# Rotating q and k out of PSUM before their norm, with shared roots and a float32 turn

## The chip, the cores and the metric

The kernel runs on one core of a Trainium2 chip. The metric is the device time of one execution in microseconds (us); lower is better. A core has TensorE (PE in the profile: matmuls and transposes; PEld is its weight load), VectorE (DVE), ScalarE (ACT), GpSimd (POOL) and the queue SP, which issues the DMA transfers. Each engine works through its own instructions in order and waits for others by semaphores. Matmuls write to PSUM; all other on-chip data is in SBUF.

## The reference, cut to what matters

One encoder layer on 1024 tokens of width 1024: a feed-forward half step, a mixer (attention beside a state-space scan), a second feed-forward half step and a gated embedding. The change is in the projection that feeds attention:

```python
u = x @ w_in[i]
q, k, v, z, xs, bm, cm, dt_raw = jnp.split(u, SPLIT_POINTS, axis=-1)
qf = _rms(q.reshape(B, S, N_Q_HEADS, HEAD_DIM).astype(jnp.float32), q_norm[i])
kf = _rms(k.reshape(B, S, N_KV_HEADS, HEAD_DIM).astype(jnp.float32), k_norm[i])
qh = _apply_rope(qf, cos, sin).astype(x.dtype)
kh = _apply_rope(kf, cos, sin).astype(x.dtype)

def _rms(xf, w):
    return xf * lax.rsqrt(jnp.mean(jnp.square(xf), axis=-1, keepdims=True) + RMS_EPS) * w
def _apply_rope(xf, cos, sin):            # pairs (x0, x1) of a head
    return jnp.stack([x0 * c - x1 * s, x0 * s + x1 * c], axis=-1).reshape(xf.shape)
```

There are 8 heads of q and 2 of k, each 64 wide. The factor of the norm is one number per token and head, so it can be multiplied in before or after the rotation; the weight of the norm is folded into the tables of sines and cosines.

## The kernel before, in words

All matmuls are done at float32 precision as three products of halves: a value is split into a high part of type float32r and the rest, `lo = value - hi` (the helper `lo`, line 87, on VectorE; the high part is a ScalarE copy), and `mm3` (lines 116 to 123, the matmul is L122) issues three matmuls for each block of 128 rows of the contraction.

`in_proj` calls `qkv_part`. Its loops run over 8 tiles of 128 tokens, first for q (`qq`, 24 matmuls of 512 columns a tile), then for k, v and dt (`kv`, 24 matmuls of 272 columns a tile). After the matmuls of tile t, `step` (lines 916 to 927) does in this order: the turn of an older tile out of the list `late`; the front of tile t (`norm`: Square on ScalarE L848, sum over each head L850, mean and epsilon L851, the root as a power of -0.5 on GpSimd L853); the low half of an older tile (L87); and the back of tile t-1 (`rope`: one Newton step on the root in `newton`, L129 to L132; the product with the root read from PSUM L860; the rotation L866 to L868; then the ScalarE copy to a high half L903 or L886).

The turn brings a tile from tokens on the partitions to head elements on the partitions. Before the change it transposes the halves: for each q head one 128x128 transposition of 64 high and 64 low columns together (L909, 8 a tile), and one copy into Q (L910); for k two heads by two halves, each written twice side by side (L892, 4 a tile), and one copy into K (L893). In Q[:, h] the upper 64 partitions hold the high half and the lower 64 the low half. K[:, g, 0] holds the high half of k on both halves of the partitions, K[:, g, 1] the low half on both, so that attention's two matmuls a product (L1159) form all four products of halves.

TensorE's order is fixed by the program: `layer.in_order` chains every TensorE instruction to the one before. The other engines' orders are made when the kernel is compiled, by a planner that walks a simulated timeline and gives each engine the instruction that is ready and comes earliest in the program. The orders are then fixed. Tiles in SBUF and PSUM come from pools with a given number of buffers; a new tile waits until the last reader of the buffer's old contents is done. Two pools of PSUM matter here: `big` (2 buffers of 1024 columns, `psb`) and `sm` (4 buffers of 512 columns, `pss`).

`kv_weights` loads and splits the weights of k and v during the last two q tiles. `tables` makes the rotation tables, two VectorE instructions (L842) and two small loads, for q ahead of its loop and for k behind the first k tile. What the step leaves over for k is put into the list `pend`, from which `xbc_gemm` pops two entries after each half of the next projection (`x0`, 2 times 24 matmuls of 512 columns, in a `big` buffer). Behind it comes `xbc_part`: a convolution out of PSUM (ScalarE L972, four VectorE taps L977, Silu L984 for each of 8 blocks), whose scratch lies where `qkv_part`'s scratch pool `qwork` lay.

Of the kernel before, what the change touches and what calls it, by code (L numbers as in the profile page):

```python
# [18 lines left out]
P = 128  # L19
# [7 lines left out]
HD = 64  # L27
# [9 lines left out]
class Layer:  # L37
# [786 lines left out]
    def qkv_part(self, c, xT):  # L824
# [20 lines left out]
        def norm(ps, nh):  # L845
            v = ps.rearrange("p (h d) -> p h d", d=HD)
            sq = wk.tile([P, nh, HD], F32, name="sq")
            nc.scalar.activation(out=sq, in_=v, func=AF.Square)  # L848
            ss = self.small.tile([P, 16], F32, name="ss")[:, :nh]
            nc.vector.reduce_sum(ss, sq, axis=AX.X)  # L850
            nc.vector.tensor_scalar(out=ss, in0=ss, scalar1=1.0 / HD, scalar2=RMS_EPS, op0=ALU.mult, op1=ALU.add)  # L851
            r = self.small.tile([P, 16], F32, name="qr")[:, :nh]
            nc.gpsimd.tensor_tensor(out=r, in0=ss, in1=self.mhalf[:, :nh], op=ALU.pow)  # L853
            return v, nh, sq, ss, r

        def rope(v, nh, m, ss, r, nm, t):

            self.newton(r, ss, nh)
            qn = wk.tile([P, nh, HD], F32, name="qn")
            nc.vector.tensor_tensor(out=qn, in0=v, in1=r.unsqueeze(2).broadcast_to([P, nh, HD]), op=ALU.mult)  # L860
            T1, T2 = (x[:, t] for x in T[nm])
            H2 = HD // 2
            for a in range(2):
                o = slice(a * H2, (a + 1) * H2)
                i = slice((1 - a) * H2, (2 - a) * H2)
                nc.vector.tensor_tensor(out=m[:, :, o], in0=qn[:, :, i], in1=T2[:, o].unsqueeze(1).broadcast_to([P, nh, H2]), op=ALU.mult)  # L866
            nc.vector.tensor_tensor(out=qn, in0=qn, in1=T1.unsqueeze(1).broadcast_to([P, nh, HD]), op=ALU.mult)
            nc.vector.tensor_tensor(out=qn, in0=qn, in1=m, op=ALU.add)  # L868
            return qn

        NK = NKV * HD
        late = []

        def kv_front(t, ps):
            nc.vector.tensor_tensor(out=self.dt[:, t], in0=ps[:, 256:272], in1=dtb, op=ALU.add)
            vv = ps[:, NK:2 * NK].rearrange("p (g d) -> p g d", d=HD)
            st = norm(ps[:, :NK], NKV)
            nc.scalar.copy(out=V[:, t, :, 0], in_=vv)
            self.lo(V[:, t, :, 1], vv, V[:, t, :, 0])
            return st  # L880

        def kv_back(t, st):

            kn = rope(*st, "k", t).unsqueeze(2).broadcast_to([P, NKV, 2, HD])
            kd = wk.tile([P, NKV, 2, 2, HD], F32R, name="qs", bufs=4)
            nc.scalar.copy(out=kd[:, :, 0], in_=kn)  # L886

            def turn():
                pt = self.pss().rearrange("p (g j t) -> p g j t", g=NKV, j=2)
                for g in range(NKV):  # L890
                    for j in range(2):
                        nc.tensor.transpose(out=pt[:, g, j], in_=kd[:, g, j].rearrange("p a d -> p (a d)").bitcast(F32), identity=self.ident)  # L892
                nc.scalar.copy(out=K[:, :, :, t * P:(t + 1) * P], in_=pt)  # L893
            late.append(turn)
            return kd[:, :, 1], kn, kd[:, :, 0]

        def q_front(t, ps):
            return norm(ps, NQ)

        def q_back(t, st):  # L900
            qs = wk.tile([P, NQ, 2, HD], F32R, name="qs", bufs=4)
            qn = rope(*st, "q", t)
            nc.scalar.copy(out=qs[:, :, 0], in_=qn)  # L903

            def turn():
# [1077 lines left out]
```

## Time and profile before

| | before |
|---|---|
| median of 3 runs | 1948.35 us (1947.01 to 1949.08) |
| the profiled execution's own time | 1948.74 us |
| its span, first to last instruction | 1946.9 us |
| granted TensorE clock | 0.998 |
| PE busy | 1927.9 us, 99% of the span |
| DVE busy | 1528.0 us, 78% |
| ACT busy | 881.1 us, 45% |
| POOL busy | 416.9 us, 21% |

The stage of the change runs from about 700 us (first q matmul) to 789 us (last k transposition) of the span. The profile's views used here are the page, the chain of waits in order of time, the busy times by window, the groups of instructions by line, the instructions of one line, the timeline of one engine, and who waited for whom. In a group's row the shapes are output <- input, partitions x elements, then the count; behind the bar stand the busy time in us, the mean of one in ns, and the engine's idle time just before them. In the chain of waits and in the timeline the first number is the start and the second the duration, in us from the span's start.

### The profile page before, as it was taken

Reading aid. Unit: us, or ns where it says so; the run is one execution under the profiler, and the core shown is the slowest. Engines: PE = TensorE matmul, PEld = TensorE weight load, DVE = VectorE, ACT = ScalarE, POOL = GpSimd, SP = SyncE. Lnnn points to the kernel's source line nnn. Section 1 sums busy time; section 2 is a strip of 40 time slices with the busy share of each in tenths; the row PEclk is TensorE's granted clock in tenths of the full one; section 3 lists DMA queues with packets and bytes.
Section 4 is the critical chain, followed back from the end, with each engine's and each line's share of the span. In section 5 each row is a group of like instructions: output and inputs, shape, how many; then the busy total and the mean of one; then the engine's idle time right before and its main releaser. Section 6 shows DMA issues by size and latency. Waiting matters only on the chain.

```text
span 1946.9 us, 25645 instructions
## 1 busy us (share of the span) xinstructions
PE 1927.9 (99%) x9132; PEld 1607.8 (83%) x9132; DVE 1528.0 (78%) x2356; ACT 881.1 (45%) x1509; POOL 416.9 (21%) x310
## 2 busy tenths in 40 slices
PE   8999999999999999999999999999999999999998
PEld 6888888888888889888888888888888888888886
DVE  7977777767678668758998878997787787877698
ACT  6433333325444224537887876633333333443311
POOL 0144535430001032001221001013444440001011
PEclk9999999999999999999999999999999999999999
DMA  8434554549866111231002663244545439976022
GB/s 296 143 125 151 190 179 156 190 159 373 297 221 212 63 42 50 84 119 68 7 1 77 212 222 121 90 165 156 190 163 178 173 121 358 331 262 226 32 77 97
DMA packets 147713, 310.34 MB, mean 159 GB/s; under 512 B 18128, under 2 KB 30800, under 8 KB 147584
## 3 DMA queue, kind: packets, MB, share of 16 engines
q1 hardware_dynamic: 147584, 308.69, 45.4%
q8 instruction: 72, 1.18, 0.2%
q14 instruction: 57, 0.47, 0.1%
HBM read 217.21 MB, written 91.42 MB: 159 GB/s over the span
## 4 chain that ended last, share of the span: by engine, by line
PE 94%; DVE 3%; DMA 1%; ACT 1%; issue 1%; POOL 0%; SPq 0%; DVEq 0%; ACTq 0%
PE sm L122 59%; PE big L516 12%; PE sm L516 9%; PE big L122 3%; PE big L1159 3%; PE sm L1181 2%; PE sm L1196 1%; PE sm L1197 1%; DMA yd<-y 1%; DVE nm L1166 1%; DVE conv L977 1%; PE sm L1270 0%; PE big L224 0%; PE sm L224 0%; PE big L909 0%
## 5 line engine op out<-in xcount | busy, mean ns | idle before, releaser
L122 PE MATMUL sm<-xh,blk 128*128 128x512 f32 x1424 | 439.8, 389 | 0.0
L122 PEld LDWEIGHTS sm<-xh,blk 128*128 128x128 f32 x1424 | 267.3, 188 | 55.4
L122 PE MATMUL sm<-xl,blk 128*128 128x512 f32 x736 | 283.8, 389 | 0.0
L122 PE MATMUL sm<-blk,xl 128*128 128x512 f32 (+2 forms) x784 | 238.2, 371 | 0.2 <-ACT xn_t L1010 0.2
L122 PE MATMUL sm<-blk,xh 128*128 128x512 f32 (+2 forms) x584 | 203.3, 379 | 1.6 <-DVE acc L1466 1.1
L108 ACT CAST blk<-raw 128x512 fp32r<-128x512 f32 (+1 forms) x168 | 101.3, 611 | 215.0 <-PE sm L122 134.1
L87 DVE TENSOR_TENSOR blk<-s,blk 128x512 fp32r<-128x512 f32 x176 | 150.8, 861 | 35.2 <-ACT blk L108 33.2
L87 DVE TENSOR_TENSOR blk<-raw,blk 128x512 fp32r<-128x512 f32 (+1 forms) x168 | 146.5, 875 | 40.6 <-ACT blk L108 40.1
L108 ACT CAST blk<-s 128x512 fp32r<-128x512 f32 x172 | 105.7, 622 | 146.5 <-PE sm L122 118.3
L122 PEld LDWEIGHTS sm<-blk,xl 128*128 128x128 f32 x784 | 142.8, 188 | 24.2 <-ACT xn_t L1010 0.5
L122 PEld LDWEIGHTS sm<-xl,blk 128*128 128x128 f32 x736 | 138.2, 188 | 28.6
L178 POOL TENSOR_TENSOR ln_k<-ln_k,mhalf 128x1 f32<-128x1 f32 x32 | 37.4, 1173 | 579.2 <-DVE ln_k L177 563.0
L516 PE MATMUL big<-xh 128*128 128x512 f32 x576 | 138.8, 390 | 0.0
L267 POOL TENSOR_TENSOR s<-raw 128x512 f32<-128x512 f32 x34 | 55.0, 1617 | 387.2 <-DVE blk L87 381.7
L87 DVE TENSOR_TENSOR xh<-blk,xh 128x1024 fp32r<-128x1024 f32 x78 | 95.4, 1223 | 48.4 <-ACT xh L462 42.3
L462 ACT CAST xl<-blk 128x1024 fp32r<-128x1024 f32 x76 | 80.2, 1055 | 113.5 <-PE sm L516 43.7
L462 ACT CAST xh<-blk 128x1024 fp32r<-128x1024 f32 x78 | 82.3, 1055 | 108.1 <-PE big L516 49.9
L122 PEld LDWEIGHTS sm<-blk,xh 128*128 128x128 f32 x584 | 109.9, 188 | 21.3 <-DVE acc L1466 1.4
L516 PEld LDWEIGHTS big<-xh 128*128 128x128 f32 x576 | 107.8, 188 | 22.2
L87 DVE TENSOR_TENSOR xl<-blk,xl 128x1024 fp32r<-128x1024 f32 x76 | 92.7, 1220 | 41.3 <-ACT xl L462 36.7
L516 PE MATMUL big<-xl 128*128 128x512 f32 x480 | 115.8, 390 | 0.0
L122 PE MATMUL sm<-xET2h,blk 128*128 128x512 f32 x352 | 108.4, 389 | 0.0
(343 smaller groups left out, 4018.5 us busy)
## 6 DMA issues: line engine op xcount, KB each, us to landing
raw<-in_wi_dram SPq DMA_DIRECT2D x81, 512.0 KB
blk<-hS SPq DMA_DIRECT2D x154, 256.0 KB
hS<-h SPq DMA_DIRECT2D x88, 256.0 KB
wr<-in_wo_dram SPq DMA_DIRECT2D x44, 512.0 KB
blk<-wT SPq DMA_DIRECT2D x88, 256.0 KB
hS<-sg SPq DMA_DIRECT2D x66, 256.0 KB
wT<-wr SPq DMA_DIRECT2D x66, 256.0 KB
blk<-in_wo_dram SPq DMA_DIRECT2D x66, 256.0 KB
```

The lines of the kernel that those rows point to most:

```text
L87: (eng or self.nc.vector).tensor_tensor(out=out, in0=full, in1=hi.bitcast(F32), op=ALU.subtract)
L108: self.nc.scalar.copy(out=b[:, 0, :n], in_=src)
L122: self.nc.tensor.matmul(ps, lhsT=a, rhs=b, start=(i == 0), stop=(i == n - 1))
L178: nc.gpsimd.tensor_tensor(out=r, in0=v, in1=self.mhalf[:, :1], op=ALU.pow)
L267: lambda: G.tensor_tensor(out=s1, in0=a21, in1=a22, op=ALU.add),
L462: A.copy(out=b[:, :, 0], in_=r)
L516: nc.tensor.matmul(ps[q], lhsT=b[:, 0, x, cut], rhs=b[:, 1, y], start=j == i == 0, stop=j == NP - 1 and i == 2)
L977: nc.vector.scalar_tensor_tensor(out=a[:, o], in0=ps[:, o.start + d - c:o.stop + d - c], scalar=cw[:, j, tap:tap + 1], in1=a[:, o], op0=AL ...
L1159: nc.tensor.matmul(ps[:, n * 512:(n + 1) * 512], lhsT=Q[:, h, q0:q0 + P], rhs=K[:, h // 4, j, n * 512:(n + 1) * 512], start=j == 0, stop=j ...
L1166: nc.vector.tensor_reduce(out=nm, in_=ps, axis=AX.X, op=ALU.max, negate=True)
L1181: nc.tensor.transpose(out=pt[:, k], in_=pr[:, kk * P:(kk + 1) * P], identity=self.ident)
L1196: nc.tensor.matmul(po, lhsT=vw, rhs=pth[k // 4][:, k % 4], start=k == 0, stop=False)
```

## The change

The order of the arithmetic changes: the unnormed q is rotated straight out of PSUM (`rope` now takes the PSUM tile), and the norm's factor is multiplied in afterwards. For q this is done by ScalarE, one instruction for each head (8 a tile); the root is taken once for two tiles (16 columns). For k, four tiles are copied to SBUF (`kraw`) and then squared, summed, rooted, rotated and scaled together (8 columns of roots, 512 columns of data); the scaling of k is one VectorE product.

The turn (`turned`) now transposes the float32 values, two heads in one 128x128 transposition: 4 a tile for q, 4 for each group of four tiles for k. The split into halves comes behind it: two ScalarE copies out of PSUM, one for each half of the partitions, and two VectorE subtractions in the step behind (`rest`). In Q the odd heads now have their high half on the lower partitions. For k the halves are then copied to the other half of the partitions by two more ScalarE copies (`then`).

The sequence is three lists. `behind`, in each step after the rotation, first runs what is left of the last turn (`los`), then the scaling of a finished group (`ready`). The scaling puts the turns into `late`, and `before`, ahead of the next step's front, takes one. So q tiles 0 and 1 are scaled in step 2 and turned in steps 4 and 5; q tiles 6 and 7 are scaled in the first k step and turned in the third and fourth; the first four k tiles are scaled in k step 4 (of 0 to 7) and turned in step 6, the last four in the pops of `x0`. The rotation table of k is made ahead of the k loop. The scratch pool's tiles change: `qs` (4 buffers) goes, `qn` has 6 buffers, and `rot`, `kraw` and `kn` come in. In the diff a longer run of removed lines is left out; the functions before stand above.

```diff
                 nc.vector.scalar_tensor_tensor(out=t_, in0=a, scalar=scale, in1=b.unsqueeze(1).broadcast_to([P, NT, HD]), op0=ALU.mult, op1=ALU.mult)
             T[nm] = (T1, T2)
 
...
+        H2, NK = HD // 2, NKV * HD
+        rows = [slice(r * HD, (r + 1) * HD) for r in range(2)]
+        Vec = nc.vector
+
+        def rope(out, v, tabs):
+            m = wk.tile([P, *v.shape[1:]], F32, name="rot")
+            flat = len(v.shape) == 3
+            T1, T2 = (x.unsqueeze(1 if flat else 2) for x in tabs)
             for a in range(2):
...
+                o, i = (slice(x * H2, (x + 1) * H2) for x in (a, 1 - a))
+                Vec.tensor_tensor(out=m[..., o], in0=v[..., i], in1=T2[..., o].broadcast_to([P, *v.shape[1:-1], H2]), op=ALU.mult)
+            Vec.tensor_tensor(out=out, in0=v, in1=T1.broadcast_to([P, *v.shape[1:]]), op=ALU.mult)
+            Vec.tensor_tensor(out=out, in0=out, in1=m, op=ALU.add)
+
+        def squares(v, ss):
+            sq = wk.tile([P, NQ, HD], F32, name="sq")
+            nc.scalar.activation(out=sq.rearrange("p h d -> p (h d)"), in_=v, func=AF.Square)
+            Vec.reduce_sum(ss, sq, axis=AX.X)
+
+        def root(ss, n):
+            ss = ss[:, :n]
+            Vec.tensor_scalar(out=ss, in0=ss, scalar1=1.0 / HD, scalar2=RMS_EPS, op0=ALU.mult, op1=ALU.add)
+            r = self.small.tile([P, 16], F32, name="qr")[:, :n]
+            nc.gpsimd.tensor_tensor(out=r, in0=ss, in1=self.mhalf[:, :n], op=ALU.pow)
+
+            def scales():
+                self.newton(r, ss, n)
+                return r
+            return scales
+
+        ready, late, los = [], [], []
+
+        def turned(pt, blocks, hi, lo, then=None):
+
+            for i, b in enumerate(blocks):
+                nc.tensor.transpose(out=pt[:, i * P:(i + 1) * P], in_=b, identity=self.ident)
+            src = [pt[rows[e]].rearrange("p (i t) -> p i t", t=P) for e in range(2)]
+            for e in range(2):
+                nc.scalar.copy(out=hi[e], in_=src[e])
+
+            def rest():
+                for e in range(2):
+                    self.lo(lo[e], src[e], hi[e])
+                if then:
+                    then()
+            los.append(rest)
+
+        def before():
+            if late:
+                late.pop(0)()
+
+        def behind():
+            if los:
+                los.pop()()
+            if ready:
+                ready.pop(0)()
+
+        kept = []
+
+        def q_turn(t, qn):
+            Qv = Q.rearrange("p (i e) s -> p i e s", e=2)[:, :, :, t * P:(t + 1) * P]
+            hi, lo = ([Qv[rows[e ^ j], :, e] for e in range(2)] for j in range(2))
+            turned(self.psb()[:, :512], [qn[:, 2 * i:2 * i + 2].rearrange("p h d -> p (h d)") for i in range(4)], hi, lo)
+
+        def q_step(t, ps):
+            before()
+            if t % 2 == 0:
+                kept.append(self.small.tile([P, 16], F32, name="ss"))
+            ss = kept[0]
+            squares(ps, ss[:, t % 2 * 8:t % 2 * 8 + 8])
+            qn = wk.tile([P, NQ, HD], F32, name="qn", bufs=6)
+            rope(qn, ps.rearrange("p (h d) -> p h d", d=HD), [x[:, t] for x in T["q"]])
+            kept.append(qn)
+            behind()
+            if t % 2:
+                _, *qns = kept
+                kept.clear()
+                scales = root(ss, 16)
+
+                def scale():
+                    r = scales()
+                    for j, q in enumerate(qns):
+                        for h in range(NQ):
+                            nc.scalar.activation(out=q[:, h], in_=q[:, h], func=AF.Identity, scale=r[:, j * 8 + h:j * 8 + h + 1])
+                    late.extend([lambda: None] * (not late) + [lambda t=t - 1 + j, q=q: q_turn(t, q) for j, q in enumerate(qns)])
+                ready.append(scale)
+
+        def kv_step(t, ps):
+            before()
+            h = t // 4
+            Vec.tensor_tensor(out=self.dt[:, t], in0=ps[:, 256:272], in1=dtb, op=ALU.add)
             vv = ps[:, NK:2 * NK].rearrange("p (g d) -> p g d", d=HD)
-            st = norm(ps[:, :NK], NKV)
+            if t % 4 == 0:
+                kept.append(wk.tile([P, 4, NK], F32, name="kraw"))
+            kr = kept[0]
+            nc.scalar.copy(out=kr[:, t % 4], in_=ps[:, :NK])
             nc.scalar.copy(out=V[:, t, :, 0], in_=vv)
             self.lo(V[:, t, :, 1], vv, V[:, t, :, 0])
...
+            behind()
+            if t % 4 == 3:
+                kept.clear()
+                ss = self.small.tile([P, 16], F32, name="ss")
+                squares(kr.rearrange("p t d -> p (t d)"), ss[:, :8])
+                scales = root(ss, 8)
+                kn = wk.tile([P, 4, NKV, HD], F32, name="kn")
+                rope(kn, kr.rearrange("p t (g d) -> p t g d", d=HD), [x[:, 4 * h:4 * h + 4] for x in T["k"]])
+                k8 = kn.rearrange("p t g d -> p (t g) d")
+                Kv = K[:, :, :, h * 512:(h + 1) * 512]
+                hi, lo = ([Kv[rows[g], g, j].rearrange("p (i t) -> p i t", t=P) for g in range(2)] for j in range(2))
+
+                def then():
+                    for g in range(2):
+                        nc.scalar.copy(out=Kv[rows[1 - g], g], in_=Kv[rows[g], g].bitcast(F32))
+
+                def scale():
+                    r = scales()
+                    Vec.tensor_tensor(out=k8, in0=k8, in1=r.unsqueeze(2).broadcast_to([P, NQ, HD]), op=ALU.mult)
+                    late.extend([lambda: None, lambda: turned(self.pss(), [kn[:, i].rearrange("p g d -> p (g d)") for i in range(4)], hi, lo, then)])
+                ready.append(scale)
 
         tables("q", HD ** -0.5)
         for t in range(NT):
             ps = self.qq(t, xT)
             if t >= NT - 2:
                 self.kv_weights(t - NT + 2)
-            step(t, ps, q_front, q_back)
+            q_step(t, ps)
+        tables("k", 1.0)
         for t in range(NT):
...
+            kv_step(t, self.kv(t, xT))
+        self.pend += [behind, before, before, behind]
         self.x0 = self.xbc_gemm(0, xT, 1)
-        assert not late and not backs and not los
+        assert not late and not ready and not los
 
     def xbc_weights(self, j):
         return [b.rearrange("p l (k c) -> p l k c", c=P) for b in self.wload(self.I["wx"][j])]
```

More of the change, by code (lines that the diff above doesn't have):

```diff
@@ L843, in tables @@
             T[nm] = (T1, T2)
[L845 to L862, printed above, removed]
-            for a in range(2):
[L864 to L869, printed above, removed]
@@ L879, in kv_front @@
             self.lo(V[:, t, :, 1], vv, V[:, t, :, 0])
[L880 to L905, printed above, removed]
-                pt = self.psb().rearrange("p (h t) -> p h t", t=P)
-                qv = qs.bitcast(F32)
-                for hh in range(NQ):
-                    nc.tensor.transpose(out=pt[:, hh], in_=qv[:, hh].rearrange("p a d -> p (a d)"), identity=self.ident)
-                nc.scalar.copy(out=Q[:, :, t * P:(t + 1) * P], in_=pt)
-            late.append(turn)
-            return qs[:, :, 1], qn, qs[:, :, 0]
```

20 lines of the change are left out of this document (removed).

## Prediction

> **What bounds the kernel now.** The page comes first, with the busy shares.
>
> ```profile
> span 1946.9 us, 25645 instructions
> PE 1927.9 (99%) x9132; PEld 1607.8 (83%) x9132; DVE 1528.0 (78%) x2356; ACT 881.1 (45%) x1509; POOL 416.9 (21%) x310
> ```
>
> PE leaves 19 us of the span, so a PE instruction taken away is worth its time as long as PE doesn't wait instead. Whether PE waits now, around the change, is in the view of who waited for whom, here PE from 700 to 960 us:
>
> ```profile
> PE sm L1119 <- ACT xn_t L1010: 0.4, 1, 0.4
> PE sm L1181 <- DVE xh L87: 0.3, 2, 0.2
> PE big L1159 <- ACT pr L1168: 0.2, 1, 0.2
> PE sm L122 <- ACT xn_t L1010: 0.2, 1, 0.2
> ```
>
> None of it lies in the stage itself. The chain of waits in order of time gives PE's pace there (start, duration):
>
> ```profile
> 741.30 5.46 PE sm L122 x24
> 746.76 0.87 PE big L909 x8
> 747.63 6.08 PE sm L122 x48
> ...
> 757.60 0.87 PE big L909 x8
> 758.47 3.01 PE sm L122 x24
> ...
> 772.29 0.44 PE sm L892 x4
> 772.73 3.01 PE sm L122 x24
> 776.18 5.47 PE big L122 x24
> ...
> 791.51 1.11 ACT conv L972
> ```
>
> A q tile is 5.46 us of matmuls, a k tile 3.01, and eight transpositions 0.87, so 0.109 each. Behind `x0` the chain leaves PE for the convolution.
>
> **The change part by part: TensorE.** The two lines' own rows count the transpositions:
>
> ```profile
> L909 PE MATMUL big<-ident,qs x64: 270/272/273, 721.2 to 762.1; 128*128 128x128 f32 x64
> L892 PE MATMUL sm<-ident,qs x32: 270/272/273, 765.2 to 788.6; 128*128 128x128 f32 x32
> ```
>
> q goes from 64 to 32, k from 32 to 8. The new ones have the same shape and type, so 56 fewer at 0.109 is 6.1 us. (I use the pace, not the 0.272 us that one takes from start to end, because they overlap.)
>
> [...]
>
> **VectorE, ScalarE and the root, in the steady state.** Rows of the groups by line, 700 to 800 us, then single lines' rows, and single rows of the timelines of ACT, POOL and DVE:
>
> ```profile
> L866 DVE TENSOR_TENSOR sq<-qn,T 128x256 f32<-128x256 f32 x16 | 6.1, 420 | 0.2
> L860 DVE TENSOR_TENSOR qn<-sm,qr 128x512 f32<-128x512 f32 x8 | 5.5, 691 | 0.7
> L868 DVE TENSOR_TENSOR qn<-qn,sq 128x512 f32<-128x512 f32 x8 | 5.5, 689 | 0.1
> L850 DVE TENSOR_REDUCE ss<-sq 128x8 f32<-128x512 f32 x8 | 5.5, 683 | 4.3 <-ACT sq L848 4.2
> L851 DVE TENSOR_SCALAR ss<-ss 128x8 f32<-128x8 f32 x8 | 1.3, 165 | 0.0
> L129 DVE TENSOR_TENSOR rs_t<-qr 128x8 f32<-128x8 f32 x8 | 1.3, 166 | 5.3 <-POOL qr L853 5.0
> L848 ACT ACTIVATE sq<-sm 128x512 f32<-128x512 f32 x8 | 4.8, 599 | 20.7 <-PE sm L122 20.7
> ...
> L1203 ACT COPY a_raw<-sm x16: 577/581/587, 906.3 to 1065.0; 64x512 f32<-64x512 f32 x16
> L1204 DVE TENSOR_TENSOR a_raw<-sm,a_raw x16: 669/689/696, 907.5 to 1065.6; 64x512 f32<-64x512 f32 x16
> ...
> 1076.47 2.04 ACT L1264 ACTIVATE xs<-xb,sdt 128x64 f32<-128x64 f32 x8
> 706.78 1.65 POOL L853 TENSOR_TENSOR qr<-ss,mhalf 128x8 f32<-128x8 f32 x1 [0.64 <-DVE ss L851]
> 723.64 2.06 POOL L853 TENSOR_TENSOR qr<-ss,mhalf 128x8 f32<-128x8 f32 x1 [3.72 <-DVE ss L851]
> 749.81 3.21 POOL L853 TENSOR_TENSOR qr<-ss,mhalf 128x8 f32<-128x8 f32 x1 [5.18 <-DVE ss L851]
> 754.53 0.70 POOL L853 TENSOR_TENSOR qr<-ss,mhalf 128x2 f32<-128x2 f32 x1 [1.50 <-DVE ss L851]
> ...
> 708.47 0.17 DVE L129 TENSOR_TENSOR rs_t<-qr 128x8 f32<-128x8 f32 x1 [1.83 <-POOL qr L853]
> 709.07 0.17 DVE L132 TENSOR_TENSOR qr<-qr,rs_t 128x8 f32<-128x8 f32 x1
> ```
>
> A new q tile costs VectorE the sum 0.68, the rotation 2.22 (two of 0.42, the product with T1 read from PSUM at L860's 0.69, the addition 0.69), two low halves on 64 partitions at L1204's 0.69 (partitions don't shorten it), and half of a mean step and four Newton steps, 0.42: 4.7 us. ScalarE pays Square 0.60, two copies at L1203's 0.58, and eight scalings with a factor per head, which L1264 does in the very form: 2.04 for eight. That is 3.8. PE's tile becomes 5.46 + 0.44 = 5.9, so both stay covered; uncovered, the scalings alone would cost 2.0 a tile.
>
> The root is now 16 columns. From 2 columns at 0.70 and 8 at 2.06, a straight line gives 3.9. The bounds come from the same line through 1.65 and through 3.21: 2.9 and 6.6. I take 3.9, since most q roots stand near 2.06.
>
> The root of 1.65 fell where VectorE did nothing but wait for it (its 1.83 of idle time ahead of L129); the others ran beside VectorE's work. [...]
>
> In the steady state all this has time: tile t of an even-odd pair ends its matmuls, and the pair's first turn is due three q tiles later, 3 x 5.9 less the last turn, 17.3 us. The q loop should run without a wait.
>
> **The border between q and k.** There the three tiles in between are k tiles. Counted from the last matmul of q tile 7, PE does three turns of 0.44 (tiles 3, 4, 5) and three k tiles of 3.01, and then wants tile 6: due at 10.35 us. What has to happen by then: Square 0.8 with its start; sum 0.68; rotation 2.22; low halves of tile 3, 1.38; mean 0.17 (all four ahead of it or beside it in the program); root 3.9; four Newton steps 0.8 at L129's 0.17 and the gaps between; eight scalings 2.04. Together 12.0, with hand-overs 12.2. PE's order is fixed, so it stands still for 1.9 us, and everything behind it on PE with it. ScalarE is not free either. By the same chain the sixteen scalings of the pair 4, 5 run from 10.2 to 14.3 us behind tile 5's last matmul, and tile 7's last is 11.8 behind that; its Square, ready at 0.2, would start at 2.5, 2.3 late. Of that 1.4 comes back, because the low halves of tile 3 are done meanwhile: 0.9. **Stall: 2.8 us.** Low bound 0: the mean taken straight behind the sum and a root of 2.9 make 7.4. High bound: Square behind all sixteen scalings and the two copies of a turn (4.1 + 1.2 + 0.6 instead of 0.8, less 1.4) with a root of 6.6 make 18.6, 8.3 late. Tile 7 follows: its scalings end 2.0 behind tile 6's, its turn is due 3.4 behind. The last k weights, and the k table's two products of 0.69 with two small loads on SP, now stand ahead of the first k tile; if that tile starts late, tile 6 is due later by as much, so nothing is added for them.
>
> **k and the tail.** The first group's chain (Square, sum, mean, root of 8, Newton, one product) takes by the same rows 0.6 + 0.68 + 0.17 + 2.06 + 0.8 + 0.69 = 5.0 and a short copy, and is due after three k tiles, 9.0: covered. The work that goes is a k tile's norm and rotation in small pieces; VectorE has less to do. The second group's turn stays the last thing in `x0`. Behind it ScalarE gets two 64-partition copies (1.16) and later two of 64x1024 for `then`, which I price by this row:
>
> ```profile
> L910 ACT CAST Q<-big 128x1024 fp32r<-128x1024 f32 x8 | 8.1, 1017 | 4.1 <-PE big L909 4.1
> ```
>
> That is 2.0 us on ScalarE, with the first convolution behind it. The convolution's taps leave ScalarE room behind it, so most is hidden; PE was 0.4 us short there already (the first row of waits), and it arrives 0.44 earlier by four transpositions. Bounds: -0.4 (that wait goes too) and 1.0 (half of the 2.0 ahead of the convolution). I take 0.3.
>
> **Sum**, against the profiled execution of 1948.74 us (1.84 around the span): -6.1 + 2.8 + 0.3 = -3.0, so 1945.7. That execution stood 0.4 above the median of the runs; against 1948.35 the forecast is **1945.3 us**.
>
> **Rivals.** (A) *No stall at the border.* For it: VectorE loses about 1 us a tile of k work, so the rows of the border may follow closer than I sum them. Against it: 12.2 against 10.35. Then -6.1 + 0.3, or from -6.5 to -5.1 with the tail's bounds: 1942.5 (1941.9 to 1943.3). [...]
>
> (B) *The border eats nearly all of it.* A root at the pace of the one at 749.81, which stood exactly there, adds 2.7: 5.5 + 0.3 - 6.1 = -0.3, 1948.0. For it: that row. Against it: the other q roots.
>
> (C) *Slower.* One mechanism: the chain from a pair's last matmul to its scaling outgrows what the turns allow, because Square queues behind sixteen scalings and the root is slow. It decides at the border from a stall of 5.8, a chain of 16.2 us; from 17.3 on the pairs before pay too. At the high bound's 18.6: the border 8.3, two earlier pairs 1.3 each, 10.9 + 0.3 - 6.1 = 5.1 more, 1953.4. Against it: it needs the worst row of each.
>
> (D) *PE gains nothing*, because what a run of transpositions costs is its change of operands and not their number. Four of L892 in 0.44 beside eight in 0.87 speak against it. It would be 2.8 + 0.3 more, 1951.4.
>
> **How the numbers follow.** Forecast 0.44 (stall 1 to 4.5: 1943.5 to 1947.0), A 0.24, B 0.17, C and D 0.15. What this measurement can tell from no change is about 0.2%, 3.9 us, so faster means below 1944.45. A lies there wholly, of the forecast's span about 0.36: 0.24 + 0.16 = 0.40. B and the rest of the forecast are the same: 0.17 + 0.28 = 0.45. C and D: 0.15. The range leaves out only C and D: 1941.6 to 1950.0, with 0.3 below A and up to a stall of 7.
>
> **What would show it.** Right: 40 transpositions of q and k; a q tile's pace of 5.9 us with no wait; PE waiting 2 to 3 us for scaled q (written by ScalarE) ahead of tile 6's turn, behind a root near 3.9; the first convolution within 1 us of its place behind `x0`. Wrong: a wait of PE within the q loop; a root over 5 us; scalings slower than 0.26 each; a wait behind 800 us that isn't there now, which would mean that fixed orders changed where nothing was edited.

## The result, and the profile after

| | before | after |
|---|---|---|
| median | 1947.96 us (4 runs beside it, 1947.01 to 1949.08) | 1958.63 us (4 runs, 1957.89 to 1960.00) |
| ratio | | 1.0056, 95% interval 1.0044 to 1.0067 |
| span of the profiled execution | 1946.9 us | 1956.6 us |
| granted TensorE clock | 0.998 | 0.996 |

The kernel after is slower by 10.7 us; the forecast was 1945.3. Of all the executions reported here and below, one (of the kernel before with four buffers for `y`) was slow, 2785.25 us at a granted clock of 0.655, and is in no ratio. The page says at once that the loss isn't work, since PE is busy 1.2 us less than before in a span that is 9.7 longer:

```profile
span 1956.6 us, 25498 instructions
PE 1926.7 (98%) x9076; PEld 1603.7 (82%) x9076; DVE 1516.4 (78%) x2266; ACT 891.1 (46%) x1566; POOL 413.5 (21%) x300
```

The transpositions are gone as the change says. The row of the new line (times in ns, then first and last start) counts 32 and 8, where 64 and 32 stood:

```profile
L880 PE MATMUL big<-ident,qn x32: 270/272/477, 727.3 to 769.7; 128*128 128x128 f32 x32
L880 PE MATMUL sm<-ident,kn x8: 270/272/302, 778.8 to 794.8; 128*128 128x128 f32 x8
```

In their place stand waits. Who waited for whom, PE from 690 to 900 us (total, times, longest):

```profile
PE sm L122 <- DVE blk L87: 4.0, 1, 4.0
PE big L880 <- ACT qn L928: 3.0, 1, 3.0
PE sm L1153 <- ACT xn_t L1044: 1.5, 1, 1.5
PE sm L880 <- DVE kn L961: 1.1, 1, 1.1
```

L928 is the scaling of q, L961 that of k, and L1153 is the transposition that had L1119 and its 0.4 before. Further on, from 900 to 1250 us, there are two that the kernel before didn't have:

```profile
PE sm L1304 <- DVE state L1318: 1.1, 1, 1.1
PE sm L1451 <- DVE y L1485: 0.4, 1, 0.4
```

And a part of the loss is no wait at all. PE by stretches (stretch, its length, PE busy and matmuls, granted clock, DMA share, GB/s), after:

```profile
727.00:747.00 20.00, 20.00 (x103) 1.00 0.03 5
747.00:750.00 3.00, 0.94 (x8) 1.00 0.66 220
750.00:754.00 4.00, 1.73 (x6) 0.56 0.20 43
754.00:758.50 4.50, 1.82 (x5) 0.50 0.58 206
758.50:762.60 4.10, 4.10 (x27) 0.73 0.01 3
```

Behind the first wait PE runs at half its clock. Of its busy time 1.73 x 0.44 + 1.82 x 0.50 + 4.10 x 0.27 = 2.8 us is lost that way. In the kernel before, the same stretches stand at 1.00.

**How the wait comes about.** PE's rows (start, duration; in brackets the idle time before and what ended it): turns of tiles 0, 1 and 2, then the first k tile, and the turn of tile 4.

```profile
727.33 0.60 PE L880 MATMUL big<-ident,qn 128*128 128x128 f32 x4
733.24 0.60 PE L880 MATMUL big<-ident,qn 128*128 128x128 f32 x4
739.15 0.60 PE L880 MATMUL big<-ident,qn 128*128 128x128 f32 x4
...
751.97 0.60 PE L122 MATMUL sm<-blk,xl 128*128 128x272 f32 x1 [4.03 <-DVE blk L87]
...
756.67 1.91 PE L880 MATMUL big<-ident,qn 128*128 128x128 f32 x4 [2.97 <-ACT qn L928]
```

Up to there the q loop runs at 5.91 us a tile, without a wait, as the forecast had it. ScalarE at the same time:

```profile
733.06 3.94 ACT L928 ACTIVATE qn<-qn,qr 128x64 f32<-128x64 f32 x16 [3.82 <-DVE qr L132]
737.02 1.17 ACT L883 CAST Q<-big 64x512 fp32r<-64x512 f32 x2
738.22 0.60 ACT L861 ACTIVATE sq<-sm 128x512 f32<-128x512 f32 x1
...
756.03 5.60 ACT L928 ACTIVATE qn<-qn,qr 128x64 f32<-128x64 f32 x23
```

The turn at 733.24 stands directly behind the last matmul of tile 5. From there tile 5's Square was ready (tile 4's starts 0.26 behind its own turn, at 727.59). It starts at 738.22, 5.0 behind the turn, since sixteen scalings of the pair 2, 3 and two copies stand ahead of it. VectorE and GpSimd:

```profile
738.23 1.39 DVE L87 TENSOR_TENSOR Q<-big,Q 64x512 fp32r<-64x512 f32 x2 [5.20 <-ACT Q L883]
...
743.49 0.17 DVE L866 TENSOR_SCALAR ss<-ss 128x16 f32<-128x16 f32 x1
...
750.54 0.18 DVE L129 TENSOR_TENSOR rs_t<-qr 128x16 f32<-128x16 f32 x1
...
751.47 0.79 DVE L87 TENSOR_TENSOR blk<-raw,blk 128x272 fp32r<-128x272 f32 x2
...
755.83 0.17 DVE L132 TENSOR_TENSOR qr<-qr,rs_t 128x16 f32<-128x16 f32 x1
```

```profile
743.74 2.90 POOL L868 TENSOR_TENSOR qr<-ss,mhalf 128x16 f32<-128x16 f32 x1 [13.44 <-DVE ss L866]
```

VectorE stood idle for 5.20 us behind the same block and then has no gap until 756.6. The mean of the pair 4, 5 came at 743.49, 10.3 us behind the turn at 733.24, its root was there at 746.64, but the four Newton steps (L129 to L132) lie among other work, from 750.54 to 755.83, in the order that was fixed at compile time. In that order the last two k weights (128x272) come at 751.47, which ends PE's 4.03, and the scaling of tile 4 can begin at 756.03, which ends its 2.97.

### The profile page after: what moved, and what is told of

Same layout as the page of the kernel before. It is cut to its first block, busy times and chain, and to the rows that moved or that the text cites. A ratio compares the mean times of both kernels' runs of the same rounds, so it can differ in the third digit from the quotient of the medians.

```text
span 1956.6 us, 25498 instructions
## 1 busy us (share of the span) xinstructions
PE 1926.7 (98%) x9076; PEld 1603.7 (82%) x9076; DVE 1516.4 (78%) x2266; ACT 891.1 (46%) x1566; POOL 413.5 (21%) x300
## 4 chain that ended last, share of the span: by engine, by line
PE 91%; DVE 4%; DMA 2%; ACT 1%; issue 1%; SPq 0%; POOL 0%; DVEq 0%; ACTq 0%
PE sm L122 57%; PE big L516 12%; PE sm L516 9%; PE big L1193 3%; PE sm L1215 2%; PE big L122 2%; PE sm L1230 1%; PE sm L1231 1%; DMA yd<-y 1%; DVE nm L1200 1%; DVE conv L1011 0%; DMA raw<-in_wx_dram 0%; DVE blk L87 0%; PE big L224 0%; PE sm L224 0%
```

## The experiments

Two theories at first. **S**: ScalarE's block of sixteen scalings is the cause. **V**: VectorE is too full at the border, whoever scales. All ratios are to the kernel before, timed beside each; its own median lay between 1947.72 and 1948.41, so two rows timed apart compare to some tenths only:

| run | median, us | ratio, 95% interval |
|---|---|---|
| q scaled on VectorE | 1950.79 | 1.0009 to 1.0028 |
| q's scaling left out | 1951.55 | 1.0009 to 1.0028 |
| root and scaling tile by tile | 1953.48 | 1.0019 to 1.0038 |
| before, with the float32 turn of q alone | 1954.80 | 1.0024 to 1.0047 |
| after, k and v weights in two loads | 1959.63 | 1.0040 to 1.0070 |
| two loads, q scaled on VectorE | 1952.41 | 1.0009 to 1.0028 |
| before, two loads | 1947.79 | 0.9986 to 1.0006 |
| two loads, VectorE, `then` on GpSimd | 1953.21 | 1.0015 to 1.0034 |
| after, turns one tile later | 1953.59 | 1.0017 to 1.0040 |
| two loads, later | 1956.26 | 1.0027 to 1.0056 |
| two loads, VectorE, later | 1949.44 | 0.9998 to 1.0017 |
| k part alone | 1947.89 | 0.9992 to 1.0011 |
| q part alone, with room | 1955.14 | 1.0021 to 1.0046 |
| k part, one K copy on VectorE | 1947.63 | 0.9987 to 1.0005 |
| k part, four buffers for y | 1946.25 | 0.9981 to 0.9998 |
| all with room, both of these | 1946.59 | 0.9982 to 1.0000 |
| before, four buffers for y | 1946.88 | 0.9986 to 1.0003 |
| k part, both | 1945.94 | 0.9980 to 0.9997 |

### Who scales q, and when

```diff
-                        for h in range(NQ):
-                            nc.scalar.activation(out=q[:, h], in_=q[:, h], func=AF.Identity, scale=r[:, j * 8 + h:j * 8 + h + 1])
+                        Vec.tensor_tensor(out=q, in0=q, in1=r[:, j * 8:j * 8 + 8].unsqueeze(2).broadcast_to([P, NQ, HD]), op=ALU.mult)
```

> The changed kernel, but each q tile is scaled by one VectorE product over 512 columns instead of eight ScalarE instructions. Theory S (sixteen scalings of 3.94 us in one block stand in ScalarE's order ahead of Square and the copies of a turn; VectorE waits for those, falls behind, and at the border the last k weights are split late): ScalarE is free, VectorE pays 0.69 a tile more (5.4 of 5.9), the 4.0 us wait for k weights and most of the 3.0 us wait for scaled q go, TensorE keeps its full clock: 1943 to 1947. Rival V (VectorE simply has too much to do around the border, because the split now takes two of its instructions a tile): more work for VectorE, so the same or worse, 1958 to 1963.

The second run drops the same two lines and puts nothing there, so it leaves the norm's factor of q out.

> The changed kernel with the scaling of q left out (q stays without its norm's factor; root and Newton steps are still computed); everything else stays. Theory S: no block on ScalarE, 1942 to 1945, no wait at the border beyond a few tenths. Rival V: VectorE's work is what it was, so its backlog at the border stays: 1954 to 1959. Rival R (the root of sixteen columns comes too late): the waits for scaled q go, the wait for the k weights stays: about 1953.

The third takes a root of 8 and the eight scalings for each tile (`root(ss, 8)`, a `scale` in every step).

> The changed kernel with q's root, Newton steps and scalings for each tile by itself: eight scalings (2.0 us) in a block instead of sixteen, half as many columns a root, twice the Newton steps; tile 7 is turned one k tile earlier. Theory S: the block is half as long, so Square and copies are late by half: 1948 to 1953. Rival P (it is the wait for two tiles that makes the first of a pair late, wherever it is scaled): tile 4 is no longer late, 1944 to 1947. Rival V: 0.4 us a tile more for VectorE, 1958 to 1962.

With the scaling on VectorE the block is gone, 3.1 us are left of the 10.7 (each against the kernel before beside it), and PE's wait for scaled q is gone. The mean of the pair 4, 5 now stands 2.8 us behind the turn of tile 1 (732.09 in this run) in place of 10.3:

```profile
734.91 0.16 DVE L866 TENSOR_SCALAR ss<-ss 128x16 f32<-128x16 f32 x1
```

One wait stays (who waited for whom, that run):

```profile
PE sm L122 <- DVE blk L87: 3.0, 1, 3.0
```

It stays at 2.4 (2.1 and 0.3) even with no scaling at all, and that run isn't faster than the one on VectorE. With eight scalings a tile the longest wait, for the same weights, is 2.8, and the time 1953.5. All three times lie between the ranges of S and of V: S names the largest part, but without the block the time of before isn't reached either. The k weights are late whoever scales, and that is V's. Of the rivals named beside these two, R (the root of 16 columns comes too late, about 1953) has the waits of the second run, but with the same root the first run has no wait for scaled q either; P (it is the waiting for a pair, 1944 to 1947) was missed by 6.5 us in the third.

### The float32 turn of q alone

The kernel before, with four transpositions of `qn` in place of eight of `qs`, two copies of 64 partitions and the low halves behind, and five buffers for `qn`; the norm, the root and k as before, so no block of scalings. The diff shows the transpositions alone.

```diff
-                for hh in range(NQ):
-                    nc.tensor.transpose(out=pt[:, hh], in_=qv[:, hh].rearrange("p a d -> p (a d)"), identity=self.ident)
+                for i in range(4):
+                    nc.tensor.transpose(out=pt[:, i * P:(i + 1) * P], in_=qn[:, 2 * i:2 * i + 2].rearrange("p h d -> p (h d)"), identity=self.ident)
```

> The kernel before, with its norm ahead of the rotation and its roots for each tile; only q's turn is changed: float32 values, four transpositions a tile, split behind it. k stays as before. 32 transpositions fewer are 3.5 us. VectorE pays one low half more (5.8 of a tile's 5.9). Theory S (no block of scalings here): 1944.5 to 1947. Rival V (the split behind the turn overloads VectorE): waits at the border like those of the changed kernel, 1950 to 1956.

1954.8, in V's range, with no scaling on ScalarE at all. The waits are at the border again, but others than in the kernel after: of the k tiles for their PSUM buffers (L860 reads them) and of a turn for its rotated q:

```profile
PE sm L122 <- DVE qn L860: 3.1, 3, 2.1
PE big L906 <- DVE qn L868: 1.2, 1, 1.2
```

### The late k weights

`kv_weights` loads the eight blocks in three parts, of three, three and two, through two raw buffers, so the third load waits until the first is split (in the kernel after it is issued at 745.58 us, behind the split that begins at 745.11). Here two loads of four blocks (and raw buffers of 1088 columns in place of 1024, not shown):

```diff
-        for k in ((0,), (3, 6))[part]:
-            n = min(3, KD - k)
+        for k in ((0,), (4,))[part]:
+            n = 4
```

> The changed kernel, but the weights of k and v come in two loads of four blocks instead of three (3, 3, 2), in buffers of 1088 columns, so that the last load waits for no earlier split to free its buffer. Theory W (the last k weights are what TensorE waits for first at the border: their load is issued only when the first split has freed a buffer, and the split's place in VectorE's fixed order is late; TensorE now comes there earlier): the wait of 4.0 us for blk goes or shrinks below 1, with it part of the clock's fall; the 3.0 us wait for scaled q stays or grows, because it was partly hidden behind the first: 1951 to 1955. Rival S (the block of scalings and nothing else): no change, 1957 to 1960.

> The same two loads, and q scaled by VectorE. Theories W and S together: no wait at the border, TensorE at full clock there: 3 us of wait less than with VectorE's scaling alone (1950.8): 1945 to 1948.5. If the wait for the weights comes back somewhere else in VectorE's order: 1949 to 1952.

> The kernel before with the same two loads: a control. It doesn't wait for these weights, so no change: 1947 to 1949 by both theories.

The wait for the weights goes (0.3 is left), and another one takes its place: the first of these runs comes to 1959.6, in the range of no change, and the second to 1952.4, just above its ranges. Who waited for whom in the kernel after with two loads, and then with q scaled on VectorE too:

```profile
PE big L881 <- ACT qn L929: 7.7, 1, 7.7
```

```profile
PE big L881 <- DVE qn L928: 4.1, 1, 4.1
```

7.7 is what 4.0 and 3.0 together were, and more: PE comes earlier to the end of the first k tile (near 748.7 us by that run's busy times by window, in the kernel after 753.70) and stands the longer ahead of the turn. With q scaled on VectorE it is tile 6 that is late, and VectorE's timeline of that run shows why (sum of tile 7, mean, Newton, scaling of 6 and 7):

```profile
747.67 0.68 DVE L863 TENSOR_REDUCE ss<-sq 128x8 f32<-128x512 f32 x1
...
752.40 0.17 DVE L867 TENSOR_SCALAR ss<-ss 128x16 f32<-128x16 f32 x1
...
757.96 0.17 DVE L130 TENSOR_TENSOR rs_t<-qr 128x16 f32<-128x16 f32 x1
...
758.95 1.29 DVE L928 TENSOR_TENSOR qn<-qn,qr 128x512 f32<-128x512 f32 x2
```

The mean starts 4.1 us behind the sum's end, after the rotation, low halves and two splits of the next stage's weights. That the loads alone were to blame fell with that. The kernel before gains nothing by two loads, so they are a fair base.

### A later turn

If the chain is just longer than the time that it has, a turn one tile later (3.4 us at the border) must take as much from the wait. (The list of turns is left out of the diff.)

```diff
-                    late.extend([lambda: None] * (not late) + [...])
+                    late.extend([lambda: None] * (2 * (not late)) + [...])
```

> The kernel after, with the turns of q one tile later (two empty places instead of one ahead of the first), so each pair's scaled q is due one tile's time later: 3.4 us at the border. Nothing is left out. Theory M (at the border the chain from the last q tile to its scaling is simply longer than the time until the turn): the wait of 3.0 for scaled q goes, and the low clock behind it; the wait of 4.0 for the last k weights stays, since nothing about it is changed: 1952.5 to 1956. Theory T (VectorE and ScalarE carry too much work there, and whichever wait is taken away, another one takes its place): 1957 to 1960, with a new wait of 2 to 4 us between 745 and 770.

> The same, and the k and v weights in two loads of four blocks each, which left one wait of 7.7 for scaled q in the run with the two loads alone (1959.6). Theory M: the wait of 7.7 falls by the 3.4 us that the turn is later, to 4.3, and with a little more of clock the time falls to 1953 to 1956.5. Theory T: 1957 to 1960.

> Two loads of k and v weights, q scaled by one VectorE product per tile, and the turns one tile later. With the first two alone the time was 1952.4 and the wait for scaled q 4.1. Theory M: that wait falls to under 1 us, the clock stays up, and the saved transpositions show at last: before less 6.1, plus the tail's 1.1 and up to 2 of new waits behind 800 us, 1943.5 to 1948. Theory T: 1950.5 to 1953.5, with another wait of 2 us or more between 745 and 770.

In the kernel after, the wait for scaled q is gone, and the time, 1953.6, is in M's range; the wait for the k weights is 2.5, where I expected 4.0, and a wait of 1.8 for a low half of Q came in. With two loads as well (1956.3, also M's) the wait of 7.7 is now, by who waited for whom,

```profile
PE big L881 <- ACT qn L929: 4.2, 1, 4.2
```

where M said 4.3. With the scaling on VectorE too, 4.1 becomes 1.5:

```profile
PE big L881 <- DVE qn L928: 1.5, 1, 1.5
PE sm L1153 <- ACT xn_t L1044: 1.5, 1, 1.5
PE sm L881 <- DVE kn L961: 1.1, 1, 1.1
```

M said under 1. The time, 1949.4, lies between M's and T's ranges: the border isn't all, since of the 6.1 us of transpositions still nothing shows.

### The k part alone, and where a lead of PE goes

The q loop of before, `kv_step` of after (`kraw` and `kn` with one buffer each, `rot` in the buffer of `sq`, and the low halves of the last q tiles in `behind`).

> The kernel before, with the changed k part alone: k turned as float32 values, four tiles at once, the parts split behind; q as it was. 24 transpositions fewer, 2.6 us. If the tail's wait ahead of the first convolution's turns comes from the k part (4 transpositions fewer directly ahead of it, and two copies out of PSUM of 64 partitions instead of one of 128), it shows here with 1.4 to 1.7 as in the kernel after, and the gain shrinks to 1.5: 1945.5 to 1948 with no wait at the border. If instead that wait comes from the q part it is 0.4 to 0.6 here and the time is 1944.5 to 1946. Theory T in its strong form (any VectorE work that moves to the border costs a wait of 2 to 4 us and clock): 1950 to 1954.

24 transpositions fewer, no wait at the border, and the time of before. PE's waits from 690 to 1250 us, the three longest; the one for `acc` has 1.1 in the kernel before too, the first had 0.4 and the last wasn't there:

```profile
PE sm L1189 <- ACT xn_t L1080: 1.8, 1, 1.8
PE sm L122 <- DVE acc L1536: 1.1, 1, 1.1
PE sm L1340 <- DVE state L1357: 0.9, 1, 0.9
```

PE comes to the last turn of k 1.7 us early (786.10, before 787.82) and has 0.4 less to do there. It gives 1.4 back ahead of L1189, where 0.4 stood before, and 0.9 at L1340. For the first wait I had thought of the two copies in `then`, and put them on GpSimd (in the run with two loads and VectorE):

```diff
-                        nc.scalar.copy(out=Kv[rows[1 - g], g], in_=Kv[rows[g], g].bitcast(F32))
+                        nc.gpsimd.tensor_copy(Kv[rows[1 - g], g], Kv[rows[g], g].bitcast(F32))
```

> As with two loads and VectorE's scaling, and the copies of k's halves to the other half of the partitions (four of 64x1024, 1.05 us each on ScalarE) are made by GpSimd. Theory T (the wait of 1.5 us ahead of the third convolution's product, 0.4 before, comes from ScalarE's added work at the end of x0): that wait is back at 0.4, 1 us less than without: 1944 to 1947.5. Rival (it comes from VectorE's two low halves, or from TensorE arriving earlier by the transpositions that went): no change against it.

The wait ahead of L1153 stayed at 1.7 and the time was 1953.2, so it isn't they. Then the q part alone with room, k as before (but with two turns in one of the k steps), and the k part with the second copy of a turn of k on VectorE:

```diff
-                nc.scalar.copy(out=hi[e], in_=src[e])
+                (nc.vector.tensor_copy if then and e else nc.scalar.copy)(out=hi[e], in_=src[e])
```

> The changed q part with the room that it needs (two loads of k and v weights, q scaled by one VectorE product per tile, turns one tile later) and k as in the kernel before. 32 transpositions fewer, 3.5 us. Theory K (the wait of 1.5 to 1.8 ahead of the turns behind the first convolution belongs to the k part): that wait is 0.4 to 0.7 here. Theory P (it grows by what PE arrives early, since VectorE and ScalarE set the pace of the convolutions): 1.5 or more, as PE arrives 2 us or more early. With a border wait of at most 2: 1946 to 1949 by both, so the wait's row decides and not the time.

> The k part alone as in the run of that name (1947.9, wait of 1.8), with the second of the two 64-partition copies of a turn of k moved from ScalarE to VectorE. Theory C (the extra copy of 0.58 delays the softplus and the convolution behind it on ScalarE): the first convolution starts about 0.6 earlier, the wait falls to 1.2 to 1.3. Theory O (the order of ScalarE's and VectorE's work within the convolutions sets it): the wait stays at 1.6 or more. Time within 1 us of 1947.9 by both.

With k as before the wait is 0.4, with the copy on VectorE 1.3 in place of 1.8 (who waited for whom in each):

```profile
PE sm L1184 <- ACT xn_t L1075: 0.4, 1, 0.4
```

```profile
PE sm L1189 <- ACT xn_t L1080: 1.3, 1, 1.3
```

So a part of it is the extra copy ahead of the convolution, as theory C had it. How large a part isn't fixed by one pair of runs. Two other pairs with and without that copy on VectorE have 1.5 against 1.7 (the k part with four buffers for `y`) and 1.3 against 1.5 (all with room), so it is 0.2 to 0.5; and in the run with 1.8, ScalarE also stood 0.27 for the load of `cw` ahead of the convolution, which the run with 1.3 doesn't. Theory P isn't ruled out: the q part alone had its own waits at the border (2.1 for scaled q, 1.9 for `rot` of k, and more), came to its last copies into K at 792.58 where before did at 788.54, and ended at 1955.1, 6 us above what both theories allowed. So PE came late to the convolution. That k's many small pieces and q's later turns don't go together would explain these waits; it isn't shown apart.

The wait for `state` follows from a store. VectorE's timeline of the k part alone, and the same of before (`y` is the tile that `yd` is stored from; it has three buffers):

```profile
1107.76 0.69 DVE L1431 TENSOR_TENSOR y<-xb,dsk 128x512 f32<-128x512 f32 x1 [2.48 <-DMA yd<-y]
```

```profile
1106.67 0.69 DVE L1361 TENSOR_TENSOR y<-xb,dsk 128x512 f32<-128x512 f32 x1 [0.56 <-DMA yd<-y]
```

Everything else on VectorE, ScalarE and PE from 830 us to here stands in the same order in both. The instruction that fills the next `y` waits for the store of an old one, 2.48 in place of 0.56 us, and `state` is behind it on VectorE. In the kernel after such waits for a store of `y` sum to 4.3 us, before to 2.1. It isn't a fixed price: in the run with one K copy on VectorE the orders behind 830 us are the same, this `y` waits 1.22, and PE doesn't wait for `state` at all. A fourth buffer:

```diff
-            y = two.tile([P, 512], F32, name="y", bufs=3)
+            y = two.tile([P, 512], F32, name="y", bufs=4)
```

> The k part alone, and four buffers in place of three for y in the left half of the scan. Theory D (the wait for state near 1111 us is a store of y that lands late and so frees its buffer late): the VectorE instruction that writes y no longer waits for a store, the wait of 0.9 for state goes, and the time is 0.5 to 1.2 lower, 1946.5 to 1947.5. If the wait stays or moves on to the next load, 1947.5 to 1948.5.

> The whole change with room: two loads of k and v weights, q scaled on VectorE, turns one tile later (1949.4 with these three), the second copy of a turn of k on VectorE, four buffers for y. If C and D hold the gains show here: 1949.4 less 0.5 less 1.0, 1947 to 1948.5. If PE's lead is taken back by whatever limits the later stages, 1949 to 1950.5.

> The kernel before with four buffers in place of three for y, nothing else. PE has no wait for state in the kernel before, so if the buffer only keeps a lead that the change gives, the time is that of before within 0.6 us, 1947.4 to 1948.7. If it is a gain of its own (with VectorE's waits for stores gone everything behind runs closer), 1946.0 to 1947.2.

> The k part alone, with the second copy of a turn of k on VectorE (1947.6 with that) and four buffers for y (1946.25 with that). If the two add up, as their places lie 300 us apart, 1945.4 to 1946.1. If PE's lead of about 3.4 us at 788 us is cut to the same size behind the convolution whatever happens ahead of it, 1946.2 to 1946.8.

The k part with it is 1.6 us faster than without, and the wait for `state` falls from 0.9 to 0.4 (who waited for whom):

```profile
PE sm L1340 <- DVE state L1357: 0.4, 1, 0.4
```

But that is the smaller part. PE's waits for `acc` (1.1) and `accr` (0.4), which the kernel before has as well, are gone too, while the `y` of the row above still waits 2.04 for its store. The kernel before with the same buffer loses its 1.1 and 0.5 there and comes to 1946.88, though its interval still holds 1. (With a fourth buffer the planner orders that stage's ScalarE and VectorE work anew, from about 1070 us on, so whether the buffer or the order does it isn't shown.) All with room, which has two loads, the scaling on VectorE, the later turns, the copy on VectorE and the buffer, stands at 1946.6, 12.0 below the kernel after and a little below both of its ranges; with the same new order it has one wait of 1.6 for `acc` left. The lowest is the k part with both, 1945.94: 1.8 us below before, a ratio of 0.9989 (0.9980 to 0.9997), and below the kernel after by 12.7. That is where the two edits should lead if they add up, but it is 0.3 below the buffer's run alone, which is within the spread of the runs. About 0.9 of the 1.8 are what the buffer gave the kernel before.

## Why the prediction was wrong

**The transpositions: right.** 40 are left, and a q tile with its turn takes 5.91 us (733.24 - 727.33) where 747.63 - 741.30 gave 6.33. All the rest of the saving came too; it was lost behind.

**"The q loop should run without a wait": right of PE, wrong of what feeds it.** The sums of 4.7 and 3.8 us a tile were averages. Sixteen scalings come as one piece; their price was right (3.94 for 16, forecast 4.1). But tile 5's Square, behind them and the copies of a turn, started 5.0 us late, VectorE lost 5.20 waiting, and at the border there is no spare time to catch up.

**The border: the step that failed.** Three things in it. First, I worked it from the last matmul of tile 7 and for tile 6 alone, and left the pair 4, 5 with a time of 17.3 us as within the loop. But tile 4's turn already stands behind a k tile: tile 5's matmuls end at 733.24, and with turns of 0.44, two q tiles of 5.46 and one k tile of 3.01 the turn is due at 748.5, 15.3 later. It came at 756.67, since the chain had been mis-sized by more than that: the prediction lets the scalings of the pair 4, 5 begin 10.2 us behind tile 5's last matmul, and they began 22.8 behind it (756.03 - 733.24). About 5 of the 12.6 came ahead of the mean, behind the block on ScalarE; 8.6 are the four Newton steps, given 0.8, which took 9.4 from the root's end at 746.64 to 756.0, because other VectorE work stands ahead of them and between them in the fixed order; the shorter root gave 1.0 back. At 10.2 tile 4 would have been in time. Second, "nothing is added for them", said of the last k weights: PE stood 4.03 us for them. That tile 6 is then due later by as much was true, and no wait of tile 6 shows, but PE's own time was lost all the same. I hadn't asked what is queued ahead of those splits on VectorE. Third, the price of the two waits, 4.03 and 2.97, wasn't their length alone: 2.8 us of slow clock came on top. In place of the forecast's 2.8 stand 4.0 + 3.0 + 2.8 = 9.8.

**The scaled tile 6 as the late one** was seen only after other things had been taken away (4.1 with two loads and VectorE). There the mechanism was as forecast, but the mean, which I had put behind the rotation and the low halves of tile 3, stood behind splits of the next stage's weights as well.

**The root: right within its bounds,** 2.90 to 3.33 us for 16 columns against 3.9 taken from 2.9 to 6.6. Three of the four stood at 3.27 to 3.33 and one, of the pair 4, 5, at 2.90. The three started beside `qn<-qn,rot` or a product for the k table (VectorE's rows at 713.82, 726.85 and 752.26), the one of 2.90 beside a low half out of PSUM (743.69). What makes the 0.4 between them isn't shown, and the stall didn't hang on it.

**k and the tail: too small.** "Covered" was said of the first group, and it was: its turn at 778.83 has no wait. The 1.1 for scaled k stand ahead of the second group's turn,

```profile
794.41 0.63 PE L880 MATMUL sm<-ident,kn 128*128 128x128 f32 x4 [1.07 <-DVE kn L961]
```

whose chain the prediction didn't sum at all: its Newton steps, from 792.77, stand on VectorE behind a split of the next stage's weights that itself waited 2.10. The tail was given 0.3 with a bound of 1.0, and the wait grew by 1.1 in the kernel after and by 1.4 in the k part alone. The `then` copies, which I had priced, weren't it; 0.2 to 0.5 is the second of the two copies out of PSUM, which I had named and not added. PE's earlier arrival by four transpositions would be another 0.4; that isn't shown apart, and the rest stays open.

**Behind 800 us:** I had said that a new wait there would mean changed orders. There are new waits (1.1 and 0.4), and the orders are the same; a store that lands later is enough (VectorE's longest wait for one of `y`, 2.64 us, stands directly ahead of the `state` that PE waits 1.1 for).

The terms again for the two spans: -6.1 + 9.8 + 1.1 for k + 1.1 in the tail + 1.5 behind = 7.4, of 9.7 measured. Of the other 2.3, 0.4 were there long before the change: PE's first matmul starts at 7.10 us of the span, before at 6.75. The remaining 1.9 are many steps below 0.5 us that I haven't followed.

**The rivals.** C was nearest, the only one to rest on Square behind all sixteen scalings and the copies, and had the sign. But it needed a slow root and the pair 6, 7, put the point of decision at 16.2 us for that pair, and came to 1953.4, 5.2 short: neither the weights nor the clock were in it. It and D had 0.15 together. A, B and D didn't happen. Two of the prediction's smaller sums are off, and nothing hangs on them: a stall of 7 would give 1949.5 and not 1950.0, and spread evenly 0.27 of the forecast's span lies below 1944.45, not 0.36.

## What to carry to other kernels

Price a step by the longest piece that an in-order engine puts ahead of it, not by busy time a tile, and go through a border between two loops with every item that is still under way, above all what the next loop's first matmul needs. In a kernel with PE at 99%, a few us that PE gains ahead of a stage can be given back at the first waits there (here 1.1 to 1.4 us ahead of the convolution, then, in some runs, about 1 behind a store that holds a buffer), so look for those waits before you count the gain. When a wait goes and the time doesn't, look for the one that took its place before you change the theory.

## What the hardware showed that I had not expected

**TensorE lost clock behind some waits and not behind others:** 2.8 us behind the 4.03 and 2.97 above, 1.7 behind a wait of 2.52, nothing behind one of 2.95. Behind the 2.52 us that the kernel after with later turns waited for its k weights (by stretches, columns as above):

```profile
747.00:749.90 2.90, 0.38 (x4) 1.00 0.42 155
749.90:751.50 1.60, 1.60 (x9) 0.68 0.32 31
751.50:753.00 1.50, 1.50 (x8) 0.50 0.71 287
753.00:755.00 2.00, 2.00 (x14) 0.78 0.30 80
```

which is 1.60 x 0.32 + 1.50 x 0.50 + 2.00 x 0.22 = 1.7 us lost. With q scaled on VectorE PE waited longer, 2.95, at the same place, and kept its clock:

```profile
748.50:750.00 1.50, 0.26 (x2) 1.00 0.00 0
750.00:752.00 2.00, 2.00 (x18) 1.00 0.44 74
```

In the run with the float32 turn of q alone PE's longest wait from 690 to 880 us was 2.1, and its clock stood at 1.00 from 755 to 760, 0.91 from 760 to 765 and 0.75 from 765 to 770; so in these runs the length of one wait isn't the measure. Why 2.52 was enough and 2.95 wasn't isn't shown, nor whether the spread of the times comes from this: runs of the kernel with later turns lie 5.1 us apart (6 runs), of the one with q scaled on VectorE 6.3 (10), of before beside the first 3.3 (21); but the four runs of the kernel after lie only 2.1 apart.
